# Layer 1's FFN by seven products, with the next layer's modulation on VectorE in two portions

## The chip, the cores and the metric

The kernel runs on one core of a Trainium2 chip. The metric is the device time of one execution in microseconds (us): three runs gave 3232.79, 3238.96 and 3241.5, so the median is 3238.96. Durations are read from one profiled execution. The engines are named as in the profile: PE multiplies matrices, DVE is VectorE, ACT ScalarE, POOL GpSimd, and SP only issues DMAs. DMAs also leave from POOL's and ACT's queues. Each engine's instructions run in a fixed order.

## The reference

Two layers of a diffusion backbone on 1024 latent tokens and 256 context tokens of width 1024. Each layer has modulation, three groups of attention heads, one output projection and a gated FFN of width 2816.

```
for i in range(DEPTH):                                    # DEPTH = 2
    mod, mod_c = silu(c) @ w_mod[i] + b_mod[i], silu(c_ctx) @ w_mod[i] + b_mod[i]
    sh1, sc1, g1, sh2, sc2, g2 = split(mod, 6)            # and sh1c ... g2c from mod_c
    h, hc = rms_norm(x)*(1+sc1)+sh1, rms_norm(xc)*(1+sc1c)+sh1c
    y, yc = token_mixers(h, hc, ...)      # gla, neighbourhood (na) and sliding-window (swa) attention, w_out
    x = x + g1*y
    x = x + g2 * ((silu(h2 @ w_gate[i]) * (h2 @ w_up[i])) @ w_down[i])    # h2: norm and sh2, sc2
    if i == 0:                                            # the context too, with g1c, g2c
        xc = xc + g1c*yc;  xc = xc + g2c * swiglu(norm(xc), ...)
return rms_norm(x, final_norm)
```

## The kernel before

Activations lie with the feature on the partitions, so a matrix of width 1024 is KD = 8 tiles; tokens fall into three blocks, B0 and B1 of 512 latents and BC of 256 context tokens. Every fp32 product is three matmuls of a high and a low part (`split`, L230 to 235: ACT copies the high part at L232, DVE subtracts at L234; `proj_T`, L436, whose matmul is L441). "Layer 1" is l = 0 in the code, "layer 2" is l = 1.

A layer runs: gla's projections (gp, gvp), gla's chain, into which the projections of swa and na are merged step by step (`merge`; the last of these are nqk, na's q and k), `swa_mix`, `na_mix`, `out_proj`, and the FFN. `na_mix` loads q, k (L803, L804) and windows of v (vw, L1039) into tiles of pool t_h, which hold the normalised input until the last projection has read it; it loads two bias tiles gm per half (L1058) and adds a table to them on POOL (L1062). A scheduler with its own timeline orders the instructions on each engine when the program is built; each engine and queue then runs in that order.

Layer 1's FFN is `ffn` (L1132). For each of NF = 22 tiles f it loads and splits three weight tiles, and for each block does 24 matmuls for gate, 24 for up, and 24 for down, whose eight sums DVE adds into x at once (L1157). Beside it `modulation_aside` (L332) computes the next layer's modulation: 96 rows of w_mod come over SP, POOL multiplies and adds them up (L342, L345, L346), DVE transposes and reduces the sums (L351, L352), and four PE matmuls (modt) bring them into place. At the end `last_norm` and the next layer's first norms follow.

Layer 2's FFN is another: `gates_seven` (L1228) replaces the eight block products of a two by two split by seven (22 jobs, product at L1286), with sums of weights made on POOL and DVE and sums of tokens on DVE; results a go to DRAM (aD). `down_blocks` (L1354) loads the rows of a back on POOL's queue (L1359), halves them on ACT and DVE (L1170, L1171), and sums over all 22 tiles in PSUM, one output tile m after the other (L1379), before the residual is added (L1398). This holds one block's a in SBUF, so w_down is loaded and split again for each block.

Of the kernel before, what the change touches and what calls it, by code (L numbers as in the profile page):

```python
# [87 lines left out]
def hybrid_layers(ctx: ExitStack, tc: tile.TileContext, A, K, out):  # L88
# [105 lines left out]
    xmD = [dr.tile([128, T], F32, name=f"xmD{k}") for k in range(KD)]  # L194
    aD = [dr.tile([128, T], F32, name=f"aD{f}") for f in range(NF)]
# [132 lines left out]

    def halves(t):
        return [t[:, 0:512], t[:, 512:1024]]  # L330

    def modulation_aside(l, u0, u1, part, sums, select):  # L332
        nu = u1 - u0
        pv4 = part[:, 0:32 * nu].rearrange("p (v b) -> p v b", v=2)
        for u in range(u0, u1):
            acc = sums()
            for k in range(KD):
                r = t_p("wm")[:, 0:512]
                SY.dma_start(r, A["w_mod"][l, 128 * k:128 * k + 128, 512 * u:512 * u + 512])
                for v in range(2):  # L340
                    if k == 0:
                        G.tensor_scalar(acc[v], r, sT[:, k, v:v + 1], None, ALU.mult)  # L342
                        continue
                    t = t_ev("mp")
                    G.tensor_scalar(t, r, sT[:, k, v:v + 1], None, ALU.mult)  # L345
                    G.tensor_tensor(acc[v], acc[v], t, ALU.add)  # L346
                if k % 2:
                    yield
            for v in range(2):
                t = t_ev("mtr")  # L350
                V.transpose(t, acc[v])  # L351
                V.tensor_reduce(pv4[:, v, 16 * (u - u0):16 * (u - u0) + 16], t.rearrange("p (b c) -> p b c", c=32),  # L352
                                axis=AX.X, op=ALU.add)
            yield
        sel = select()
        G.memset(sel, 0.0)
        for g in range(4):
            r = slice(32 * g, 32 * g + 32)
            V.tensor_copy(rev(sel[r], 0, [[160, 4], [1, 32]]), ident[r, r].unsqueeze(1).to_broadcast([32, 4, 32]))
        tp = p_c("modt")  # L360
        for q in range(4):
            PE.matmul(tp[:, 0:8 * nu], sel[:, 128 * q:128 * q + 128],
                      part[:, 0:32 * nu].rearrange("p (m q) -> p q m", q=4)[:, q], start=(q == 0), stop=(q == 3))
        V.tensor_tensor(modT[l][:, :, 4 * u0:4 * u1], tp[:, 0:8 * nu].rearrange("p (v j) -> p v j", v=2),
                        bmT[:, 48 * l + 4 * u0:48 * l + 4 * u1].unsqueeze(1).to_broadcast([128, 2, 4 * nu]), ALU.add)
        for w in range(2):
            if u0 <= 6 * w + 3 < u1:
                mod_vectors(l, w)
        yield


# [116 lines left out]
    def gla(l, hh, hl, ctx_out, before, given):  # L488
# [8 lines left out]
        def gproj(items, put, with_ctx, given=()):  # L497
            given = list(given)
            w = given + [None] * (len(items) - len(given))
            for blk in blks:  # L500
# [570 lines left out]
    def out_proj(l, blks):  # L1071
# [9 lines left out]
        def part(grp):  # L1081
# [6 lines left out]
            for m in range(KD):  # L1088
                w = wcols(A["w_out"][l], 128 * m)
                for o, n in grp:  # L1090
# [6 lines left out]
                    if len(blks) == 2:  # L1097
                        G.dma_start(xmD[m][:, o:o + n], x[m][:, o:o + n])
# [3 lines left out]
        def norms():  # L1102
            for blk in blks[:-1]:
# [3 lines left out]
                for k in range(KD):  # L1107
                    xv, pool = x[k][:, blk[0]:blk[0] + blk[1]], k % 2 == 1
                    if len(blks) == 2:
                        scaled(l, xv, r, k, yh, yl, blk)  # L1110
                    else:
                        modulate(l, 1, xv, r[:, :blk[1]], k, yh, yl, blk, pool)
                    yield
        run(merge(part(blks[-1:]), norms(), 1, 2))
        rs = block_rstd(ss, blks[-1])
        if len(blks) == 2:
            return x, yh, yl, rs
        rs = rs()
        return x, yh, yl, lambda: run(norm_block(l, 1, x, rs, yh, yl, blks[-1]))
# [12 lines left out]
    def ffn(l, x, hh, hl, blks, last):  # L1132
        ss, add = square_sums(x, blks)
        for f in range(NF):
            wg = wcols(A["w_gate"][l], 128 * f)
            wu = wcols(A["w_up"][l], 128 * f)
            r = t_raw("wd", [128, D])
            SY.dma_start(r, A["w_down"][l, 128 * f:128 * f + 128, :])
            wd = split(r, "wd", [128, D])
            for o, n in blks if f < NF - 1 else last:  # L1140
                pg = p_a("pg")
                proj_T(wg, hh, hl, (o, n), pg)
                pu = p_a("pu")
                proj_T(wu, hh, hl, (o, n), pu)
                a = t_w2("a")
                S.activation(a[:, :n], pg[:, :n], AF.Silu)  # L1146
                V.tensor_tensor(a[:, :n], a[:, :n], pu[:, :n], ALU.mult)
                ah, al = t_w2("ah", dt=F32R), t_w2("al", dt=F32R)
                S.activation(ah[:, :n], a[:, :n], AF.Copy)  # L1149
                V.tensor_tensor(al[:, :n], a[:, :n], ah[:, :n].bitcast(F32), ALU.subtract)  # L1150
                yield (f, (o, n), None)
                v = 1 if o == 1024 else 0
                for m in range(KD):
                    pd = either(p_b, p_c, "pd")
                    for i, (w, b) in enumerate(((wd[0], ah), (wd[0], al), (wd[1], ah))):
                        PE.matmul(pd[:, :n], w[:, m * 128:(m + 1) * 128], b[:, :n], start=(i == 0), stop=(i == 2))  # L1156
                    V.scalar_tensor_tensor(x[m][:, o:o + n], pd[:, :n], modT[l][:, v, 40 + m:41 + m],  # L1157
                                           x[m][:, o:o + n], ALU.mult, ALU.add)
                    if f == NF - 1 and last is blks:
                        add(m, (o, n))  # L1160
                yield (f, (o, n), ss)

# [11 lines left out]
    def token_sums(l, x, yh, yl, rs, ops):  # L1174
# [34 lines left out]
        for k in range(4):  # L1209
            t1, v22 = half(x[k], 0), half(x[k + 4], 1)  # L1210
            V.tensor_tensor(t1, v22, t1, ALU.subtract)
            j = 2 * k
# [9 lines left out]
        for k in range(4):  # L1222
            t2, v21 = half(x[k], 0), half(x[k + 4], 0)
            V.tensor_tensor(v21, v21, t2, ALU.subtract)
# [3 lines left out]
    def gates_seven(l, x, yh, yl, rs):  # L1228
        order = ("b11", "b21", "t1", "t3", "t2", "b22", "t4")
        jobs = [(f, w) for f in range(0, NF, 2) for w in ("w_gate", "w_up")]  # L1230
        early = 4
# [19 lines left out]
        def weights():  # L1251
# [4 lines left out]
            for j, (f, name) in enumerate(jobs):  # L1256
# [13 lines left out]
                yield made(s3)  # L1270
                yield made(a22)
# [3 lines left out]
        def product(i, bank, start):  # L1275
            w, b = ready.pop(0), ops[order[i]]
            new = next(feed, None)
            if new is not None:
                ready.append(new)
            for k in range(4):  # L1280
                wv = [t.rearrange("p (k f) -> p k f", f=128)[:, k] for t in w]
                for q, (p, m) in enumerate(((0, 0), (0, 1), (1, 0))):
                    pieces = b[k][m] if isinstance(b[k][m], list) else [b[k][m]]
                    n = 512 // len(pieces)
                    for c, v in enumerate(pieces):
                        PE.matmul(bank[:, n * c:n * c + n], wv[p], v, start=(start and k == 0 and q == 0),  # L1286
# [313 lines left out]
```

## Time and profile before

| what | value |
|---|---|
| median of three runs | 3238.96 us |
| the profiled execution | 3235.02 us, its span 3233.2 |
| PE busy | 3067.4 us, 95% |
| DVE, POOL, ACT busy | 53%, 34%, 32% |
| layer 1's FFN, 885 to 1835 us | PE busy for 938.75 of 950 |
| layer 2's FFN, 2515 to 3233 us | PE busy for 430.64 of 446, then 256.96 of 272 |

The span is the time from the first to the last instruction that the profile records; what the execution has beyond it lies around it. A window of the profile lists for a stretch of the span how long each engine was busy; PEclk is the granted share of TensorE's full clock. The chain is the succession of work that ended last, each piece with its start and length. A group of instructions by line has its busy time, the mean length of one in ns, the idle time in front of them and what ended that.

### The profile page before, as it was taken

Reading aid. Unit: us, or ns where it says so; the run is one execution under the profiler, and the core shown is the slowest. Engines: PE = TensorE matmul, PEld = TensorE weight load, DVE = VectorE, ACT = ScalarE, POOL = GpSimd, SP = SyncE. Lnnn points to the kernel's source line nnn. Section 1 sums busy time; section 2 is a strip of 40 time slices with the busy share of each in tenths; the row PEclk is TensorE's granted clock in tenths of the full one; section 3 lists DMA queues with packets and bytes.
Section 4 is the critical chain, followed back from the end, with each engine's and each line's share of the span. In section 5 each row is a group of like instructions: output and inputs, shape, how many; then the busy total and the mean of one; then the engine's idle time right before and its main releaser. Section 6 shows DMA issues by size and latency. Waiting matters only on the chain.

```text
span 3233.2 us, 50611 instructions
## 1 busy us (share of the span) xinstructions
PE 3067.4 (95%) x19726; PEld 2613.5 (81%) x19726; DVE 1726.4 (53%) x3431; ACT 1044.3 (32%) x1976; POOL 1087.8 (34%) x938
## 2 busy tenths in 40 slices
PE   7998999889999999999999899999989899999998
PEld 5887877677878888888888789887868688887877
DVE  3255444566675666666555724545766644444342
ACT  4332223455321111111111432224664444333231
POOL 1011020230189888887000101110411376655010
PEclk8999999999999999999999898999999999999999
DMA  7233455764312222222111223356555232225452
GB/s 251 84 125 104 126 160 156 209 186 155 92 62 72 82 79 82 79 82 66 40 40 38 76 66 98 95 155 184 148 172 171 69 101 79 79 85 170 143 187 80
DMA packets 371543, 365.80 MB, mean 113 GB/s; under 512 B 65100, under 2 KB 297512, under 8 KB 371304
## 3 DMA queue, kind: packets, MB, share of 16 engines
q1 hardware_dynamic: 358296, 318.79, 32.6%
q0 software_dynamic: 11856, 39.59, 3.8%
q10 hardware_dynamic: 1152, 4.19, 0.3%
q8 instruction: 155, 2.54, 0.3%
q14 instruction: 84, 0.69, 0.1%
HBM read 285.86 MB, written 76.64 MB: 112 GB/s over the span
## 4 chain that ended last, share of the span: by engine, by line
PE 72%; DMA 5%; DVE 4%; issue 3%; POOL 2%; ACT 1%; SPq 0%; DVEq 0%; ACTq 0%; POOLq 0%
PE q L1286 10%; PE pg L441 9%; PE pd L1156 9%; PE pu L441 9%; PE pd L1379 7%; PE op L441 6%; PE nqk L441 4%; PE ptp L849 3%; PE swp L448 2%; PE gp L441 1%; PE nao L863 1%; PE swo L863 1%; DMA wm<-in_w_mod_dram 1%; PE nvp L448 1%; PE gvp L448 1%
## 5 line engine op out<-in xcount | busy, mean ns | idle before, releaser
L1157 DVE SCALAR_TENSOR_TENSOR x<-pd,modT,x 128x512 f32<-128x512 f32 (+1 forms) x528 | 317.9, 655 | 195.0 <-PE pd L1156 192.9
L345 POOL TENSOR_SCALAR mp<-wm,sT 128x512 f32<-128x512 f32 x168 | 283.8, 1701 | 42.0 <-DVE mpart L352 35.9
L1286 PE MATMUL q<-yh,ws 128*128 128x512 f32 (+1 forms) x1056 | 282.9, 356 | 4.4 <-DVE us L1346 2.6
L1379 PE MATMUL pd<-ha,wdh 128*128 128x512 f32 (+1 forms) x748 | 225.2, 384 | 5.3 <-ACT ha L1170 2.2
L346 POOL TENSOR_TENSOR macc<-macc,mp 128x512 f32<-128x512 f32 x168 | 224.1, 1360 | 0.0
L830 ACT ACTIVATE P<-P,m 128x640 f32<-128x640 f32 (+2 forms) x216 | 167.2, 775 | 137.4 <-DVE m L826 131.4
L1286 PEld LDWEIGHTS q<-yh,ws 128*128 128x128 f32 x1056 | 183.3, 190 | 34.8 <-ACT ws L1170 5.6
L234 DVE TENSOR_TENSOR wcl<-wr,wch 128x1024 fp32r<-128x1024 f32 x98 | 140.7, 1435 | 124.1 <-ACT wch L232 122.5
L441 PE MATMUL pg<-yh,wch 128*128 128x512 f32 (+1 forms) x528 | 187.9, 356 | 1.0 <-ACT a L1146 1.0
L441 PE MATMUL pg<-yl,wch 128*128 128x512 f32 (+1 forms) x528 | 187.9, 356 | 0.0
L441 PE MATMUL pg<-yh,wcl 128*128 128x512 f32 (+1 forms) x528 | 187.4, 355 | 0.0
L441 PE MATMUL pu<-yl,wch 128*128 128x512 f32 (+1 forms) x528 | 187.1, 354 | 0.0
L441 PE MATMUL pu<-yh,wcl 128*128 128x512 f32 (+1 forms) x528 | 187.0, 354 | 0.0
L441 PE MATMUL pu<-yh,wch 128*128 128x512 f32 (+1 forms) x528 | 186.9, 354 | 0.0
L232 ACT ACTIVATE wch<-wr 128x1024 fp32r<-128x1024 f32 x100 | 106.0, 1060 | 245.3 <-PE pg L441 89.9
L1156 PE MATMUL pd<-al,wdh 128*128 128x512 f32 (+1 forms) x528 | 184.9, 357 | 0.0
L1156 PE MATMUL pd<-ah,wdl 128*128 128x512 f32 (+1 forms) x528 | 184.7, 357 | 0.0
L1286 PE MATMUL q<-yl,ws 128*128 128x512 f32 (+1 forms) x528 | 173.8, 356 | 0.4 <-DVE yl L1189 0.4
L1379 PEld LDWEIGHTS pd<-ha,wdh 128*128 128x128 f32 x748 | 139.9, 192 | 35.2 <-ACT ha L1170 3.8
L849 PE MATMUL ptp<-ident,P 128*128 128x128 f32 x984 | 144.5, 286 | 10.0 <-DVE pT L855 7.8
L1156 PE MATMUL pd<-ah,wdh 128*128 128x512 f32 (+1 forms) x528 | 148.6, 356 | 0.3 <-ACT ah L1149 0.3
L1379 PE MATMUL pd<-ha,wdl 128*128 128x512 f32 (+1 forms) x374 | 143.5, 384 | 0.8 <-DVE wdl L234 0.7
(351 smaller groups left out, 7809.9 us busy)
## 6 DMA issues: line engine op xcount, KB each, us to landing
wm<-in_w_mod_dram SPq DMA_DIRECT2D x96, 256.0 KB
wr<-in_w_gate_dram SPq DMA_DIRECT2D x46, 512.0 KB
wr<-in_w_up_dram SPq DMA_DIRECT2D x46, 512.0 KB
wm<-in_w_mod_dram POOLq DMA_DIRECT2D x32, 512.0 KB, 4.7
wr<-in_w_out_dram SPq DMA_DIRECT2D x32, 512.0 KB
wr<-in_w_down_dram SPq DMA_DIRECT2D x32, 512.0 KB
k<-naD SPq DMA_DIRECT2D x48, 320.0 KB
gm<-in_const_nam_dram SPq DMA_DIRECT2D x24, 576.0 KB
```

Source lines behind the costliest of these rows:

```text
L232: S.activation(h, raw, AF.Copy)
L234: engine.tensor_tensor(l, raw, h.bitcast(F32), ALU.subtract)
L345: G.tensor_scalar(t, r, sT[:, k, v:v + 1], None, ALU.mult)
L346: G.tensor_tensor(acc[v], acc[v], t, ALU.add)
L441: PE.matmul(pt[:, :n], a[:, k, :], b[k][:, o:o + n], start=(k == 0 and i == 0), stop=(k == KD - 1 and i == 2))
L448: PE.matmul(pt[:, :n], a[k][:, t * 128:(t + 1) * 128], b[:, k % 2, c0:c0 + n], start=(k == 0 and i == 0), stop=(k == KD - 1 and i == 2))
L830: exps[:] = [S.activation(P, P, AF.Exp, bias=m[:, i:i + 1], scale=-1.0, accum_out=sums[:, i:i + 1])]
L849: line[:] = [PE.transpose(tp[:, (cc * 2 + i) * 128:(cc * 2 + i + 1) * 128], pr[i][:, (c + cc) * 128:(c + cc + 1) * 128], ident)]
L1156: PE.matmul(pd[:, :n], w[:, m * 128:(m + 1) * 128], b[:, :n], start=(i == 0), stop=(i == 2))
L1157: V.scalar_tensor_tensor(x[m][:, o:o + n], pd[:, :n], modT[l][:, v, 40 + m:41 + m], x[m][:, o:o + n], ALU.mult, ALU.add)
L1286: PE.matmul(bank[:, n * c:n * c + n], wv[p], v, start=(start and k == 0 and q == 0), stop=(k == 3 and q == 2), skip_group_check=not start)
L1379: PE.matmul(pt[:, 0:n], w[i][:, f - f0, :], hs[f][b][:, c0:c0 + n], start=(f == 0 and q == 0), stop=(f == NF - 1 and q == 2))
```

## The change

Layer 1 now uses the seven products too. `gates_seven` takes the context along: its 256 columns are multiplied plainly by the four weight pieces a11, a12, a21 and a22, into a bank of their own, 48 matmuls a job, and the results are stored over SP. Since a bank more is in use, three jobs start early instead of four.

`down_next` is the new second half: blocks B0, B1 and BC one after the other, each with all weights of w_down loaded and split again; rows of the next x leave from ACT's queue, sums of squares go along. In the context block `norms()` fetches those rows for B0 and B1 on POOL's queue and normalises them beside the products, so that layer 2 starts its gp on B0. The context's own norm is layer 2's first job. `out_proj` stores its x to DRAM in both layers.

`modulation_aside` on POOL goes. `modulation_behind` does the products on DVE, one operation for a multiplication with its addition, and takes rows of w_mod over POOL's queue. Portion 1 (512-column pieces 0 to 3 of w_mod, for latents and context) runs beside the blocks B0 and B1 of down. Portion 2 (pieces 4 to 11, for latents only) runs in layer 2 as every third step of the projections.

```diff
+    def modulation_behind(l, u0, u1, row, sums, wide, ahead, every):
...
+                G.dma_start(r, A["w_mod"][l, 128 * k:128 * k + 128, 512 * u:512 * u + 512])
...
+            for v in range(nv):
+                if k == 0:
+                    V.tensor_scalar(acc[v], r, sT[:, k, v:v + 1], None, ALU.mult)
+                else:
+                    V.scalar_tensor_tensor(acc[v], r, sT[:, k, v:v + 1], acc[v], ALU.mult, ALU.add)
+            if k == KD - 1:
+                for v in range(nv):
+                    t = wide("mtr")[:, 0:512]
+                    V.transpose(t, acc[v])
+                    V.tensor_reduce(pv4[:, v, 16 * (u - u0):16 * (u - u0) + 16],
+                                    t.rearrange("p (b c) -> p b c", c=32), axis=AX.X, op=ALU.add)
+            if k % every == every - 1:
+                yield
...
+    def down_next(l):
+        def sums(m, hs, n, pt):
+            for f0 in range(0, NF, KD):
+                nf = min(KD, NF - f0)
+                r = t_raw("wr", [128, KD, 128])
+                SY.dma_start(r[:, 0:nf], A["w_down"][l][128 * f0:128 * (f0 + nf), 128 * m:128 * m + 128]
+                             .rearrange("(k p) f -> p k f", p=128))
+                w = split(r[:, 0:nf], "wd", [128, nf, 128])
+                for f in range(f0, f0 + nf):
+                    for q, (i, b) in enumerate(((0, 0), (0, 1), (1, 0))):
+                        PE.matmul(pt[:, 0:n], w[i][:, f - f0, :], hs[f][b], start=(f == 0 and q == 0),
+                                  stop=(f == NF - 1 and q == 2))
+        def take(f, o, n, dst):
+            r = t_w2("ar")[:, 0:n]
+            G.dma_start(r, aD[f][:, o:o + n])
+            halve(dst, r)
...
+            for m in range(KD):
+                pt = either(p_a, p_b, "pd")
+                sums(m, hs, n, pt)
+                V.scalar_tensor_tensor(xs[m], pt[:, 0:n], modT[l][:, v, 40 + m:41 + m], xs[m], ALU.mult, ALU.add)
+                if blk != BC:
+                    S.dma_start(xD[l + 1][:, m, o:o + n], xs[m])
...
+                if m in steps:
+                    for _ in range(steps[m]):
+                        next(aside, None)
...
+        aside = modulation_behind(l + 1, 0, 4, t_w2, sums_of, t_ev, 3, 2)
+        for o in (0, 512):
...
+            rqs.append(block((o, 512), hs, xs, aside, {m: 2 for m in range(1, 6)}))
...
+        def norms():
+            for rq, (o, n) in zip(rqs, (B0, B1)):
+                rs = across(rq, n)
+                for k in range(KD):
+                    xv = t_w2("xn")
+                    G.dma_start(xv, xD[l + 1][:, k, o:o + n])
+                    modulate(l + 1, 0, xv, rs, k, hh, hl, (o, n), False)
...
+        def context(w, half, bank):               # in gates_seven
+            for k in range(4):
+                for q, (p, y) in enumerate(((0, yh), (0, yl), (1, yh))):
+                    PE.matmul(bank[:, 0:C], w[k][p], y[4 * half + k][:, T:N], start=(half == 0 and k == 0 and q == 0),
+                              stop=(half == 1 and k == 3 and q == 2))
...
+            rest = modulation_behind(l, 4, 12, t_w2, lambda: [t_ev("macc")], t_ev, 1, 2)
         proj = merge(proj, rest, 2, 1)
         run(merge(chain(), proj, 1, 1, False))
         run(merge(seq(finish(), swa_mix(l, ctx_out)), proj, 1, 1))
         run(na_mix(l, ctx_out))
-        x, hh, hl, last_norm = out_proj(l, blks)
-        if not ctx_out:
-            gates_seven(l, x, hh, hl, last_norm)
+        x, hh, hl, rs = out_proj(l, blks)
+        gates_seven(l, x, hh, hl, rs, ctx_out)
+        if ctx_out:
+            hh, hl, last_norm = down_next(l)
```

The first place is POOL's order in layer 2 between the end of `swa_mix` and the start of `na_mix`: gm is a bias tile of na, yD a stored row of attention output. Before:

```order
L965 DMA yD_0_158<-ys_21537 64x512 x2
L1062 TENSOR_TENSOR gm_22211<-gm_22211,gt_22193 128x384 x3
L965 DMA yD_512_159<-ys_21751 64x512 x2
L965 DMA yD_0_158<-ys_21955 64x512 x2
L1062 TENSOR_TENSOR gm_22216<-gm_22216,gt_22202 128x384 x3
L1062 TENSOR_TENSOR gm_22358<-gm_22358,gt_22193 128x384 x3
L1062 TENSOR_TENSOR gm_22363<-gm_22363,gt_22202 128x384 x3
```

POOL's order at the same place now, with wm the rows of w_mod of portion 2:

```order
L1326 DMA wm_21807<-in_w_mod_dram 128x512
L1018 TENSOR_TENSOR gm_21927<-gm_21927,gt_21913 128x384 x3
L1326 DMA wm_21810<-in_w_mod_dram 128x512
L1018 TENSOR_TENSOR gm_22069<-gm_22069,gt_21904 128x384 x3
L1018 TENSOR_TENSOR gm_22074<-gm_22074,gt_21913 128x384 x3
L1326 DMA wm_21813<-in_w_mod_dram 128x512
L1326 DMA wm_21816<-in_w_mod_dram 128x512
L1326 DMA wm_21819<-in_w_mod_dram 128x512
L1326 DMA wm_21825<-in_w_mod_dram 128x512
```

The issues of rows now stand among the adds, and the last eleven (these four and seven more) behind nine adds that wait for loads of na.

The second place is PE's order at the end of `swa_mix` and the first tile of `na_mix`: swo are values of swa, sc and sl scores of na. Before:

```order
L863 MATMUL swo_22027<-pT_22120,vsw_20538 64x128 x4
L863 MATMUL swo_22027<-pT_22127,vsw_20538 64x128
L883 MATMUL rrt_22137<-ident,bc_22129 128x128 x4
L863 MATMUL swo_22027<-pT_22127,vsw_20538 64x128 x3
L849 MATMUL ptp_22275<-ident,P_22224 128x128
L849 MATMUL ptp_22275<-ident,P_22225 128x128
L808 MATMUL sc_22280<-k_4036_22163,q_22157 128x256
```

PE's order there now, with modt the four matmuls that end portion 2:

```order
L819 MATMUL swo_21549<-pT_21710,vsw_19709 64x128 x4
L819 MATMUL swo_21549<-pT_21717,vsw_19709 64x128
L839 MATMUL rrt_21727<-ident,bc_21719 128x128 x4
L819 MATMUL swo_21549<-pT_21717,vsw_19709 64x128 x3
L1359 MATMUL modt_21859<-mpart_17765,sel_21853 128x32 x4
L764 MATMUL sc_21934<-k_3830_21874,q_21868 128x256
L765 MATMUL sc_21934<-k_3831_21875,q_21868 128x256
```

Before, na's first tile (ptp, of its probabilities) was already under way between the last rows of swa; now no matmul of na stands in front of modt. The last nqk stands 38 rows further up in this order, with the scores and values of two swa tiles between.

The third place is DVE's order at the end of layer 1's FFN. Before, the last sums and the next layer's norm rows (nt, yl) take turns:

```order
L1157 SCALAR_TENSOR_TENSOR x_8274<-pd_17071,modT_113,x_8274 128x512
L419 TENSOR_SCALAR nt_17024<-nt_17024,av_116,modT_114 128x512
L424 SCALAR_TENSOR_TENSOR yl_8266<-nt_17029,modT_114,yh_8258 128x512
L1157 SCALAR_TENSOR_TENSOR x_8276<-pd_17087,modT_113,x_8276 128x512
L420 TENSOR_TENSOR yl_8265<-nt_17024,yh_8257 128x512
L422 SCALAR_TENSOR_TENSOR nt_17038<-x_8276,av_116,rs_17018 128x512
```

DVE's order in the context block of down now, about one output tile m:

```order
L234 TENSOR_TENSOR wdl_16370<-wr_16366,wdh_16368 128x768
L234 TENSOR_TENSOR wdl_16411<-wr_16407,wdh_16409 128x1024
L1398 SCALAR_TENSOR_TENSOR xm_15773<-pd_16305,modT_113,xm_15773 128x256
L378 SCALAR_TENSOR_TENSOR nt_16396<-xn_16394,av_116,rs_16291 128x512
L378 SCALAR_TENSOR_TENSOR nt_16402<-xn_16400,av_116,rs_16291 128x512
L234 TENSOR_TENSOR wdl_16441<-wr_16437,wdh_16439 128x1024
L1406 TENSOR_TENSOR ss_15775<-ss_15775,sq_16391 128x256
L380 SCALAR_TENSOR_TENSOR hl_15765<-nt_16396,modT_114,hh_15757 128x512
L380 SCALAR_TENSOR_TENSOR hl_15766<-nt_16402,modT_114,hh_15758 128x512
L234 TENSOR_TENSOR wdl_16471<-wr_16467,wdh_16469 128x768
```

Three splits of weights (wdl) now stand in every m, and the four norm operations of two rows between them.

## Rows read from the trace of the kernel before

**Rows 1.** The page: its first part (busy us, share, instructions), and the chain by line.

```profile
PE 3067.4 (95%) x19726; PEld 2613.5 (81%) x19726; DVE 1726.4 (53%) x3431; ACT 1044.3 (32%) x1976; POOL 1087.8 (34%) x938
...
PE q L1286 10%; PE pg L441 9%; PE pd L1156 9%; PE pu L441 9%; PE pd L1379 7%; PE op L441 6%; PE nqk L441 4%; PE ptp L849 3%; PE swp L448 2%; PE gp L441 1%; PE nao L863 1%; PE swo L863 1%; DMA wm<-in_w_mod_dram 1%; PE nvp L448 1%; PE gvp L448 1%
```

**Rows 2.** Windows by stage: us, PE, PEld, DVE, ACT, POOL, PEclk, DMA, GB/s.

```profile
885.00:1835.00 950.00, 938.75 (x4884) 807.50 (x4883) 588.01 (x865) 167.91 (x249) 560.78 (x379) 0.99 0.21 68
...
2515.00:2961.00 446.00, 430.64 (x2124) 364.58 (x2122) 218.27 (x266) 179.37 (x309) 261.16 (x177) 0.98 0.27 85
2961.00:3233.00 272.00, 256.96 (x1186) 211.48 (x1186) 108.55 (x141) 80.09 (x123) 34.31 (x53) 0.97 0.47 150
```

**Rows 3.** Windows inside the stages, columns as above.

```profile
2221.00:2316.00 95.00, 85.72 (x841) 72.03 (x839) 66.26 (x229) 58.34 (x142) 14.94 (x20) 1.00 0.61 163
2316.00:2420.00 104.00, 93.64 (x913) 79.86 (x912) 68.51 (x221) 65.65 (x147) 29.39 (x34) 0.96 0.58 167
...
1802.00:1855.00 53.00, 42.95 (x200) 35.01 (x199) 42.23 (x65) 23.42 (x39) 11.46 (x13) 0.88 0.28 102
...
2585.00:2909.00 324.00, 323.49 (x1611) 275.82 (x1612) 150.41 (x172) 128.98 (x222) 207.31 (x140) 0.99 0.27 86
...
2962.00:3105.00 143.00, 140.25 (x596) 112.84 (x597) 64.98 (x79) 48.78 (x68) 28.65 (x45) 0.98 0.56 177
```

**Rows 4.** The chain in order of time: start, length, what.

```profile
915.62 5.44 PE pg L441 x24
...
931.94 2.87 PE pg L441 x24
...
957.01 5.44 PE pg L441 x24
...
1854.38 46.02 PE gp L441 x192
...
2585.51 323.20 PE q L1286 x1608
```

**Rows 5.** Timeline of PE where the first FFN begins: start, length, what.

```profile
886.69 0.28 PE L441 MATMUL pg<-yh,wch 128*128 128x256 f32 x1
```

**Rows 6.** The instructions on tile gp in layer 2, one kind of three.

```profile
L441 PE MATMUL gp<-yh,wch x112: 277/389/797, 1802.4 to 1899.6; 128*128 128x512 f32 x96, 128*128 128x256 f32 x16
```

**Rows 7.** Waits of PE at layer 2's FFN start: total, times, longest.

```profile
PE q L1286 <- ACT ws L1170: 6.4, 1, 6.4
```

**Rows 8.** DMAs of the page's part 6, and the landing of L1359's.

```profile
wm<-in_w_mod_dram POOLq DMA_DIRECT2D x32, 512.0 KB, 4.7
...
DMA to landing us min/median/max: 3.2/5.1/8.9
```

**Rows 9.** Groups by line, 2962 to 3215 us: busy, mean ns, idle before.

```profile
L234 DVE TENSOR_TENSOR wdl<-wr,wdh 128x1024 fp32r<-128x1024 f32 x30 | 36.7, 1224 | 47.0 <-ACT wdh L232 46.1
...
L232 ACT ACTIVATE wdh<-wr 128x1024 fp32r<-128x1024 f32 x30 | 31.7, 1059 | 77.6 <-PE pd L1379 64.9 <-DMA wr<-in_w_down_dram 6.9 <-DMA out_dram<-fo 4.1
...
L1359 POOL DMA_DIRECT2D ar<-aD x40 | 21.6, 540 | 103.3 <-DVE ha L1171 100.4 <-DMA ar<-aD 1.9
...
L1398 DVE SCALAR_TENSOR_TENSOR xm<-pd,modT,xm 128x512 f32<-128x512 f32 x15 | 11.2, 750 | 28.2 <-PE pd L1379 27.9 <-DMA xm<-xmD 0.3
```

**Rows 10.** Groups of POOL and of DVE, 885 to 1835 us.

```profile
L345 POOL TENSOR_SCALAR mp<-wm,sT 128x512 f32<-128x512 f32 x168 | 283.8, 1701 | 42.0 <-DVE mpart L352 35.9 <-DMA wm<-in_w_mod_dram 4.3 <-DVE yl L420 1.1
...
L351 DVE STREAM_TRANSPOSE mtr<-macc 128x512 f32<-128x512 f32 x24 | 16.8, 701 | 0.0
```

**Rows 11.** The instructions on tiles nqk and swo: count, ns, first and last start.

```profile
L441 PE MATMUL nqk<-yh,wch x120: 278/389/501, 2118.2 to 2219.7; 128*128 128x512 f32 x96, 128*128 128x256 f32 x24
...
L863 PE MATMUL swo<-pT,vsw x422: 272/273/324, 2220.8 to 2315.8; 128*64 128x128 f32 x141
```

**Rows 12.** Timelines of SP's queue and of POOL: start, length, what.

```profile
2227.18 15.43 SPq L1039 DMA_DIRECT2D vw<-vD  x15
...
2309.31 8.89 POOL L1062 TENSOR_TENSOR gm<-gm,gt 128x384 f32<-128x384 f32 x9 [7.51 <-PE sl L809]
```

More of the change, by code (lines that the diff above doesn't have):

```diff
@@ L325, in modulation @@
             yield
[L329 to L369, printed above, removed]
     def square_sums(x, blks):
@@ L1130, in parts @@
         V.scalar_tensor_tensor(dst[1], v, b, dst[0].bitcast(F32), ALU.add, ALU.subtract)
[L1132 to L1161, printed above, removed]
     def t_x(s, dt=F32R):
@@ L1273, in gates_seven, with take @@
         ready = [next(feed) for _ in range(3)]
-        def product(i, bank, start):
-            w, b = ready.pop(0), ops[order[i]]
+        def take():
+            w = ready.pop(0)
             new = next(feed, None)
@@ L1279, in product @@
                 ready.append(new)
+            return [[t.rearrange("p (k f) -> p k f", f=128)[:, k] for t in w] for k in range(4)]
+        def product(i, bank, start):
+            w, b = take(), ops[order[i]]
             for k in range(4):
-                wv = [t.rearrange("p (k f) -> p k f", f=128)[:, k] for t in w]
                 for q, (p, m) in enumerate(((0, 0), (0, 1), (1, 0))):
@@ L1347, in gates_seven, with rows @@
             done(j, 1)
-            product(6, pd, False)
+            if ctx_too:
+                bank = p_b("qc")
+                context(take(), 0, bank)
+            w = product(6, pd, False)
+            if ctx_too:
+                context(w, 1, bank)
+                context_done(j, 1, bank)
             V.tensor_tensor(result(j, 2), u2, pd, ALU.add)
             done(j, 2)
+    def modulation_behind(l, u0, u1, row, sums, wide, ahead, every):
+        nu, nv = u1 - u0, 2 if u0 == 0 else 1
+        part = wk.tile([128, 128], F32, tag="mac", name=nm("mpart"), bufs=1)
+        pv4 = part[:, 0:16 * nu * nv].rearrange("p (v b) -> p v b", v=nv)
+        todo = [(u, k) for u in range(u0, u1) for k in range(KD)]
+        def rows():
+            for u, k in todo:
+                r = row("wm")[:, 0:512]
+                G.dma_start(r, A["w_mod"][l, 128 * k:128 * k + 128, 512 * u:512 * u + 512])
+                yield r
+        feed, ready, acc = rows(), [], None
+        for u, k in todo:
+            while len(ready) < ahead:
+                r = next(feed, None)
+                if r is None:
+                    break
+                ready.append(r)
+            r = ready.pop(0)
+            if k == 0:
+                acc = sums()
+            for v in range(nv):
+                if k == 0:
+                    V.tensor_scalar(acc[v], r, sT[:, k, v:v + 1], None, ALU.mult)
+                else:
+                    V.scalar_tensor_tensor(acc[v], r, sT[:, k, v:v + 1], acc[v], ALU.mult, ALU.add)
[7 more added lines that the diff above has]
+                yield
+        sel = wide("sel")[:, 0:512]
+        V.memset(sel, 0.0)
+        for g in range(4):
+            r = slice(32 * g, 32 * g + 32)
+            V.tensor_copy(rev(sel[r], 0, [[160, 4], [1, 32]]), ident[r, r].unsqueeze(1).to_broadcast([32, 4, 32]))
+        tp = p_c("modt")
+        n = 4 * nu * nv
+        for q in range(4):
+            PE.matmul(tp[:, 0:n], sel[:, 128 * q:128 * q + 128],
+                      part[:, 0:4 * n].rearrange("p (m q) -> p q m", q=4)[:, q], start=(q == 0), stop=(q == 3))
+        V.tensor_tensor(modT[l][:, 0:nv, 4 * u0:4 * u1], tp[:, 0:n].rearrange("p (v j) -> p v j", v=nv),
+                        bmT[:, 48 * l + 4 * u0:48 * l + 4 * u1].unsqueeze(1).to_broadcast([128, nv, 4 * nu]), ALU.add)
+        w = 0 if u0 == 0 else 1
+        for v in range(nv):
+            V.scalar_tensor_tensor(av[l][:, w, v], modT[l][:, v, 24 * w + 8:24 * w + 16], 1.0,
+                                   pv[:, 16 + 16 * w + 8 * l:24 + 16 * w + 8 * l], ALU.add, ALU.mult)
+        yield
```

153 lines of the change are left out of this document (96 added, 57 removed).

## The prediction

> **What bounds the kernel now.** I read the page's first part, then the chain by line, then the chain in order of time, and last the windows of the stages that the change touches. The page has PE busy for 3067.4 of 3233.2 us, DVE for 53%, POOL for 34%, and the chain's dearest lines are the FFN products of both layers [rows 1]. In layer 1's FFN PE is busy for 938.75 of 950 us [rows 2]: that stage lasts as long as its matmuls, so fewer of them are worth their time there. Layer 2's middle is another case: from the last projections to the end of swa_mix PE works 85.72 of 95 us, then in na_mix 93.64 of 104 [rows 3]. There a load or a row of VectorE that comes late is felt at the end.
>
> In the chain 24 pg matmuls of 512 columns take 5.44 us and 24 of 256 take 2.87 [rows 4]: 0.2267 and 0.1196 each. One matmul on all three blocks costs 2 x 0.2267 + 0.1196 = 0.573.
>
> **Layer 1's FFN, before.** From its first matmul at 886.69 [rows 5] to the end of layer 2's gp at 1854.38 + 46.02 = 1900.40 [rows 4] there are 1013.7 us. One f is 72 matmuls on each block, 72 x 0.573 = 41.26; the chain has 957.01 - 915.62 = 41.39 from one f to the next [rows 4], 910.5 for 22. gp has three kinds of 96 matmuls of 512 and 16 of 256 [rows 6], 71.0. What is left, 32, is loss, nearly all where the last block's sums, its norm and gp follow on each other: PE is busy for 42.95 of 53 us there, at a granted clock of 0.88 [rows 3].
>
> **Gate and up, after.** Each of 22 jobs has 7 products of 12 matmuls of 512, and 48 of 256 for the context: 84 x 0.2267 + 48 x 0.1196 = 24.78, 545.2 in all, where 22 x 48 x 0.573 = 605 stood: -60. That jobs of this kind hold such a rate is seen in layer 2: 96 matmuls a job (72 of 512, 24 of 256) are 19.19 by the prices above, and 1608 of them, 16.75 jobs, take 323.20 [rows 4], 19.30 a job. Its stage lasts 446 [rows 2] against 22 x 19.19 = 422: 24 lost, most of it at the start, where the longest single wait is 6.4 for ScalarE's first pieces [rows 7]. Here three early jobs hold 3 x (24 x 0.2267 + 48 x 0.1196) = 33.5 us of products for that time, layer 2's four 21.8. I take 22 (14 to 28).
>
> **Down, after.** 8 x 22 x 3 x 0.573 = 302.5, as before. Its losses are new to this layer, and layer 2's rows bound them: 596 matmuls, 135 us, in the first 143 [rows 3], so 8 lost about the first block; 7 from B0 to B1, the rest of what its stage of 272 [rows 2] has over 239.4 of products and the last norm's share; 6 from B1 to the context, 3 for transfers. In the context block weights may bind: it loads all of w_down again, 24 groups for 8 x 66 x 0.1196 = 63.1 of PE, and has two raw buffers, each held from issue until DVE's split. A transfer of 512 KB takes 4.7 [rows 8], ScalarE's part 1.06, DVE's 1.22 [rows 9]: 6.98 for two in flight, 3.49 a group. The third group, of six, comes to three quarters, 2.62: 16 x 3.49 + 8 x 2.62 = 77, 14 over PE. With two STTs of 0.75 [rows 9] ahead of each split it is 4.24 and 3.37, 95, 32 over; with prefetch that holds, 0. DVE's order there has two or four STTs of norm rows between splits (order of DVE in the section on the change): I take 18. Down's losses: 42.
>
> gp stays 71.0, with 4 in front of it. Sum 545.2 + 22 + 302.5 + 42 + 71.0 + 4 = 986.7: -27. With nothing lost in the context block and 14 in gates it is -53; with 32 there, 28 in gates and 6 more at the ends of blocks, -1.
>
> **Modulation, portion 1, and what goes.** POOL's 168 products of 1.70 us [rows 10] and the adds that belong to them go; they lay under PE, so nothing is gained. Portion 1 is 64 STTs of some 0.75 and 8 transposes of 0.70 [rows 10] with reduces that I take at as much, 59 us of DVE, beside B0's and B1's 239 of products. DVE has 48 splits (54), 44 halves at half a split (27) and 16 sums (12) there: 152 in all, so nothing. Without that cover it would cost as far as a split waits behind two steps, 1.5 us at a time, 15 for ten. xD's store at layer 2's head goes, and its rows leave from ScalarE's queue under PE: nothing either way.
>
> **Portion 2, at the seam from swa_mix to na_mix.** Here the change adds a wait. 64 rows of w_mod on POOL's queue and 64 STTs are dealt out among layer 2's projections; the projections last longer in the order, and the last nqk stands only two swa tiles before the end of swa (orders of PE and POOL in the section on the change). Before, nqk's last matmul began at 2219.7 and swo's at 2315.8 [rows 11]. 422 of the swo fall into 95 us [rows 11], 20 a tile, 4.5 us each: now PE is through some 8.5 us after the last nqk, which I call +0. na's q, k and v take the tiles that it frees. On SP the last 15 of 16 vw began 7.5 us after it and took 15.43 [rows 12], so gm's loads leave at +23.5 and land, at the 5.1 of a row of aD [rows 8], at +29. POOL's adds of gm stand in front of the last 11 rows of w_mod: three triples, nine adds of 0.99 [rows 12] and one row's issue between, done at +38.5. Six buffers are free: issues of 0.54 [rows 9] and landing bring the sixth row at +47, slots come free from +44.9, and the last row lands at +53.4; its STT, transpose, reduce and sel end at +56. PE's order has modt, which needs them, in front of na's first scores. So PE stands from +8.5 to +56: 47. At least it is 37 (gm in by +20), at most 60 (rows at 8.9).
>
> Against that: the swa tiles that now have projections beside them lose less of the 9.3 us of [rows 3], 6 back; na starts with its loads all there, 4 back of 10.4. The chain of gla, ahead, has less to fill it with: one step in three of what is merged into it is now without matmuls, +7. The middle comes to +44; at the most 60 with 5 more of chain, +65; with the wait hidden, 0 to +5.
>
> **A rule against the queue.** The rows of aD, issued from POOL while DVE halves and splits, landed in 3.2 to 8.9 us, 5.1 in the middle [rows 8]. The Trainium skill, "SBUF — State Buffer", section "SBUF: two separate sides", says that GpSimd itself writes the descriptors of a DMA issued from its queue, through a port that VectorE's operations can lock it out of, so that such a DMA seems slow. The trace has the spread and not its reason. If it bites, both batches at the seam land at 8.9 and not at 5.1, 2 x 3.8 = +7.6.
>
> **Sum.** -27 + 44 = +17: 3235.02 + 17 = 3252 for the profiled run (span 3233.2, 1.8 around it). The three runs have a median 3.9 above it: 3256.
>
> **Rivals.**
> *Seam hidden* (0.30; the one that is faster): rows and na's loads are in before swa ends, and the middle costs +3. It decides when the last row of w_mod lands by +10. For it: the DMA engines are busy for 0.61 of that time [rows 3], and swa's last tiles may themselves run slower. Against: three queues in a row (SP's vw, POOL's adds, the rows). 3239 - 27 + 3 = 3215.
> *Context block starved* (0.16): weights and norm rows hold each other up; the xn rows come on POOL's queue, and a late one stops the split behind it. FFN gives -5 and not -27, and gla's chain loses 7 more: 3256 + 22 + 7 = 3285. It decides at over 4.2 us a group. For it: 3.4 of splits and 3.0 of STTs of 7.9 us of PE per m. Against: layer 2's first block of down has DVE at 65 of 143 [rows 3], and PE keeps on.
> *The rate doesn't hold* (0.07): the fifth weight piece a21 and the context's results make a job wait 0.7 us: 22 x 0.7 = 15, 3271. Layer 2's jobs have POOL busy 207 and DVE 150 of 324 us [rows 3], so there is room.
> *Slow rows*, as above (0.05): 3256 + 7.6 = 3264.
>
> **How the numbers follow.** The forecast has 0.42, its own range 3239 to 3275. Under 0.3%, 10 us, a measurement of this kernel can't be told from no change: faster is below 3229, slower above 3249. Of the forecast 0.04 falls to faster, 0.16 to same, 0.22 to slower; of the hidden seam 0.27 and 0.03 (same); the others have 0.03 same and 0.25 slower. Sums: 0.31, 0.22, 0.47. The range 3205 to 3284 leaves out a third of the hidden seam and half of the starved block.
>
> **What would show it.** A job of layer 1's gates at 24.8 to 25.3 us; the context block of down at 63 (prefetch holds), 77 to 82 (mine) or over 95; a hole of PE of over 35 us in front of modt, ended by DVE, with POOL's adds of gm ahead of the last rows. No hole means the seam is hidden; a hole that a wait of another kind ends, that I have named the wrong queue. Wrong altogether would be a job over 27, or FFN above 1014.

## The result, and the profile after

The changed kernel takes 3328.53 us in the median of four runs (3318.81 to 3335.92), the kernel before 3240.23: a ratio of 1.028, 95% interval 1.0264 to 1.0297. It is slower, the sign forecast, by 88 us and not by 17. The profiled execution took 3335.92, its span 3334.1. It was the slowest of the four, so the stretches below add up to a span 101 us longer and not to 88. PE is busy for less than before; this is the first line of the page, against [rows 1]:

```profile
PE 3036.3 (91%) x19470; PEld 2583.6 (77%) x19470; DVE 1672.4 (50%) x3278; ACT 1201.7 (36%) x2258; POOL 876.6 (26%) x931
```

So waiting grew. Windows of the changed kernel, columns as in [rows 2]: the gates of layer 1, blocks B0 and B1 of down, its context block; then gla's chain with swa's and na's projections, the time between swa and na, and na.

```profile
890.00:1452.00 562.00, 553.73 (x2920) 476.09 (x2918) 270.38 (x317) 202.72 (x353) 254.42 (x180) 0.99 0.23 71
1452.00:1705.00 253.00, 246.20 (x1074) 200.96 (x1073) 157.94 (x224) 82.94 (x117) 54.83 (x95) 0.99 0.67 210
1705.00:1789.00 84.00, 70.60 (x546) 67.48 (x544) 53.28 (x76) 39.02 (x55) 11.82 (x22) 0.98 0.68 202
...
1910.00:2165.00 255.00, 217.06 (x1964) 195.71 (x1964) 142.53 (x339) 56.28 (x123) 48.50 (x70) 0.85 0.42 124
2325.00:2394.00 69.00, 2.52 (x14) 2.28 (x12) 22.02 (x36) 0.35 (x1) 19.82 (x30) 0.53 0.79 215
2394.00:2520.00 126.00, 98.72 (x937) 85.14 (x936) 73.82 (x241) 70.33 (x157) 26.71 (x30) 0.88 0.55 162
```

The FFN's three windows are as full as forecast. Below them PE stands for 38 of 255 us, for all of 69 at a granted clock of 0.53 (near the lower of its two levels, 1.2 of 2.4 GHz), and for 27 of 126. The tiles gp, nqk and swo give the borders, against [rows 6, 11]:

```profile
L397 PE MATMUL gp<-hh,wch x112: 283/389/629, 1789.3 to 1866.5; 128*128 128x512 f32 x96, 128*128 128x256 f32 x16
...
L397 PE MATMUL nqk<-hh,wch x120: 277/389/504, 2153.5 to 2314.6; 128*128 128x512 f32 x96, 128*128 128x256 f32 x24
...
L819 PE MATMUL swo<-pT,vsw x456: 272/273/324, 2163.8 to 2325.0; 128*64 128x128 f32 x152
```

| stretch | before | after | difference |
|---|---|---|---|
| start to the end of gp | 1900.4 | 1867 | -33 |
| end of gp to the last swo | 415.4 | 458 | +43 |
| last swo to the first matmul of na, on its own | hidden | 69 | +69 |
| from there (before: from the last swo) to out_proj | 107.8 | 125.8 | +18 |
| out_proj to the end | 809.6 | 814.6 | +5 |

In the first of the two middle stretches the last nqk now begins at 2314.6, 10 us before the end of swo, as the order had shown. What waits in gla's chain is in the waits of PE and then of POOL and DVE, 1910 to 2165 us (total, times, longest):

```profile
PE ket L593 <- DVE ke L589: 9.6, 5, 3.1
PE bp L572 <- DMA lac<-laD: 5.9, 3, 4.7
PE op L635 <- DVE sx L618: 4.9, 5, 1.9
PE at L628 <- DVE am L649: 4.7, 3, 3.1
```

```profile
...
POOL wm L1326 <- PE op L635: 37.0, 3, 18.8
...
POOL am L646 <- DVE macc L1342: 11.0, 4, 7.4
```

```profile
DVE macc L1342 <- DMA wm<-in_w_mod_dram: 14.0, 8, 4.0
```

POOL stands with a row's issue until PE's op has read one of the chain's tiles and so freed a buffer of t_w2; DVE then stands for the row. am and ke belong to the chain and stand behind them. At the seam, the timelines of SP, of POOL and of PE and the chain answer to [rows 12] (in brackets the idle time before, and what ended it):

```profile
2324.95 24.38 SPq L995 DMA_DIRECT2D vw<-vD  x16
2349.74 1.34 SPq L1014 DMA_DIRECT2D gm<-in_const_nam_dram  x3
```

```profile
2355.51 2.88 POOL L1018 TENSOR_TENSOR gm<-gm,gt 128x384 f32<-128x384 f32 x3 [16.91 <-issue]
2358.34 0.57 POOL L1326 DMA_DIRECT2D wm<-in_w_mod_dram  x1
2358.93 5.72 POOL L1018 TENSOR_TENSOR gm<-gm,gt 128x384 f32<-128x384 f32 x6
2364.61 2.67 POOL L1326 DMA_DIRECT2D wm<-in_w_mod_dram  x5
```

```profile
2391.77 1.92 PE L1359 MATMUL modt<-mpart,sel 128*128 128x32 f32 x8 [66.48 <-DVE sel L1355]
```

```profile
2366.74 14.89 DMA wm<-in_w_mod_dram
2381.72 0.76 DVE macc L1342
...
2382.77 5.46 DMA wm<-in_w_mod_dram
...
2391.77 1.92 PE modt L1359 x8
```

That is the chain forecast, link by link: vw, gm, nine adds, the last rows, modt. Two links are longer. The 16 vw go out in 24.38 us, where 15 took 15.43 before, so gm's loads leave 35 us after the last nqk and not 23.5. The last rows take up to 14.89 us and not 5.1, while na's loads for its second pair of heads are under way. In na a second hole follows. POOL's adds wait for the second half of the biases; the store of ys stands behind them on POOL's queue; and ScalarE's copy pT waits for the buffer of t_w2 that this store holds, and PE for pT (windows, the chain, PE's and ScalarE's waits from 2420 to 2446):

```profile
2424.00:2434.00 10.00, 0.04 (x2) 0.00 (x0) 0.32 (x3) 0.00 (x0) 4.76 (x6) 0.72 0.89 255
2434.00:2444.00 10.00, 0.00 (x0) 0.00 (x0) 0.00 (x0) 0.09 (x1) 1.48 (x3) 0.50 1.02 248
```

```profile
2424.89 4.09 DMA gm<-in_const_nam_dram
...
2431.13 3.78 POOL gm L1018 x4
2434.91 8.91 DMA yD<-ys
```

```profile
ACT pT L809 <- DMA yD<-ys: 21.6, 1, 21.6
...
PE nao L819 <- ACT pT L809: 20.3, 1, 20.3
```

### The profile page after: what moved, and what is told of

It reads as the page before. It is cut to its first block, busy times and chain, and to the rows that moved or that the text cites. A ratio compares the mean times of both kernels' runs of the same rounds, so it can differ in the third digit from the quotient of the medians.

```text
span 3334.1 us, 50957 instructions
## 1 busy us (share of the span) xinstructions
PE 3036.3 (91%) x19470; PEld 2583.6 (77%) x19470; DVE 1672.4 (50%) x3278; ACT 1201.7 (36%) x2258; POOL 876.6 (26%) x931
## 4 chain that ended last, share of the span: by engine, by line
PE 76%; DMA 9%; DVE 5%; issue 4%; POOL 2%; ACT 2%; SPq 1%; ACTq 0%; DVEq 0%; POOLq 0%
PE q L1217 22%; PE pd L1380 7%; PE pd L1485 7%; PE op L397 6%; PE nqk L397 5%; PE gp L397 5%; PE swp L404 4%; PE qc L1225 4%; DMA wm<-in_w_mod_dram 3%; PE ptp L805 3%; PE nvp L404 3%; PE gvp L404 2%; PE swo L819 1%; PE nao L819 1%; DMA wr<-in_w_down_dram 1%
## 5 line engine op out<-in xcount | busy, mean ns | idle before, releaser
L1217 PE MATMUL q<-yh,ws 128*128 128x512 f32 (+1 forms) x1760 | 515.0, 370 | 5.9 <-DVE us L1303 2.7
L1217 PE MATMUL q<-t,ws 128*128 128x512 f32 x1320 | 321.1, 394 | 17.8 <-ACT t L1080 6.9
L1217 PEld LDWEIGHTS q<-t,ws 128*128 128x128 f32 x1320 | 248.4, 190 | 71.2 <-ACT t L1080 7.7
L1091 DVE TENSOR_TENSOR ws<-s,ws 128x512 fp32r<-128x512 f32 x176 | 184.1, 1047 | 176.3 <-ACT ws L1090 173.4
L1091 DVE TENSOR_TENSOR ws<-wr,ws 128x512 fp32r<-128x512 f32 x154 | 143.2, 933 | 195.6 <-ACT ws L1090 195.4
L234 DVE TENSOR_TENSOR wdl<-wr,wdh 128x1024 fp32r<-128x1024 f32 (+1 forms) x120 | 138.7, 1157 | 190.7 <-ACT wdh L232 162.3
L1380 PE MATMUL pd<-ha,wdh 128*128 128x512 f32 x704 | 220.1, 393 | 5.6 <-ACT wdh L232 2.9
L1217 PEld LDWEIGHTS q<-yl,ws 128*128 128x128 f32 x880 | 160.7, 190 | 25.0 <-DVE yl L1109 0.7
L1250 POOL TENSOR_TENSOR us<-us,gs 128x512 f32<-128x512 f32 x88 | 139.8, 1597 | 113.2 <-DVE us L1257 102.8
L1225 PE MATMUL qc<-yh,ws 128*128 128x256 f32 x704 | 140.4, 283 | 0.0
```

What stands on the lines that cost most here:

```text
L234: engine.tensor_tensor(l, raw, h.bitcast(F32), ALU.subtract)
L1091: V.tensor_tensor(dst[1], v, dst[0].bitcast(F32), ALU.subtract)
L1217: PE.matmul(bank[:, n * c:n * c + n], w[k][p], v, start=(start and k == 0 and q == 0), stop=(k == 3 and q == 2), skip_group_check=not start)
L1225: PE.matmul(bank[:, 0:C], w[k][p], y[4 * half + k][:, T:N], start=(half == 0 and k == 0 and q == 0), stop=(half == 1 and k == 3 and q == 2))
L1250: G.tensor_tensor(c, c, gates.pop((j - 1, i)), ALU.mult)
L1380: PE.matmul(pt[:, 0:n], w[i][:, f - f0, :], hs[f][b], start=(f == 0 and q == 0), stop=(f == NF - 1 and q == 2))
```

## The experiments

Theory 1: portion 2 in layer 2's middle is the whole loss, because its rows hold up queues and buffers that PE waits for. The rivals: the new FFN, the spreading of the projections, DVE's time, the DMA engines. Times are medians of four or more runs; the kernel before had 3236.9 to 3239.3 beside them.

**Without portion 2.** `rest = iter(())`, constants in modT and av.

> Leaves out portion 2 of the modulation: its columns of modT and av are filled with constants. Theory 1 (portion 2 in layer 2's middle is the whole loss, about 43 us in gla's chain and swa, 69 at the seam, 18 in na): the middle goes back to the kernel before, nqk ends near 2190, and the time is about 3200 (3190 to 3212), faster than before by the 33 us of the FFN. Rival (the new second half of layer 1's FFN, its stores and its other order of gp make the chain slow): 3290 or more, with PE at a granted clock under 0.9 from 1920 to 2120 us as now.

3198.59, ratio 0.9884 (0.9859 to 0.9908): the FFN is worth 38 us, and portion 2 cost 130. The 38 are net: in the profiled executions gp ends 46 us earlier than before, and from there to the end it is 10 us longer.

**Empty steps.** `rest = iter((None,) * 33)`.

> Leaves out the work of portion 2 (constants in its place) but keeps its 33 steps, empty, among the projections, so the projections are spread as in the changed kernel. If the rows and STTs hold up DVE and POOL (theory 1), the chain loses at most 10 us against the run without steps, and only the late nqk is left, a hole of 25 to 30 us in front of na: about 3235. If the spreading itself costs the chain its cover (rival), the chain from 1867 to the end of swa takes some 455 us as now: about 3270 to 3290.

3207.16, a miss: no hole is left in front of na. The spreading costs 9 us, little more than the runs spread (3191 to 3206 without steps, 3204 to 3211 with them). And it doesn't move nqk: its last matmul begins 96 us before the last swo, as before the change. The stretches from 53 us behind gp on, changed kernel and then empty steps:

```profile
1920.00:2120.00 200.00, 167.62 (x1610) 149.23 (x1612) 116.93 (x289) 37.62 (x87) 34.51 (x58) 0.83 0.40 118
```

```profile
1912.00:2112.00 200.00, 188.63 (x1751) 169.00 (x1750) 101.96 (x263) 45.39 (x98) 20.96 (x34) 0.96 0.40 113
```

The DMA share is the same, 0.40; PE's work is not.

**Products without rows, rows without products.** The first reads the resident unit matrix in place of r, the second lets DVE touch 32 columns of each row.

```diff
-                r = row("wm")[:, 0:512]
+                if nv == 1:
+                    yield ident.unsqueeze(1).to_broadcast([128, 4, 128])
+                    continue
```

> Leaves out the loads of portion 2: all its 64 products, transposes, reduces and modt are made as in the changed kernel, on the resident unit matrix in place of rows of w_mod. If rows and their buffers are the price (theory 1), nqk ends some 95 us before swa does, as without portion 2, and 64 STTs cost 5 to 15 us beside empty steps: 3210 to 3225. If DVE's time in its queue is the price (rival), the chain stays as long as now: 3270 and above.

> Leaves out the products of portion 2, but for 32 of the 512 columns of each row: all rows are loaded over POOL's queue into t_w2 as in the changed kernel, and DVE touches each briefly. Theory 1: nearly all of the loss stays, nqk ends within 15 us of swa, a hole of 50 to 70 us in front of na: 3300 to 3330. Rival (DVE's time): 3225 to 3250.

3223.49 and 3331.55. Against 3207.16 with empty steps DVE's 57 us of work cost 16, the rows alone 124. The last nqk of the first begins 107 us before the last swo; that of the second 14, and the hole in front of na is 92 us, more than the 50 to 70 expected. nqk of both:

```profile
L397 PE MATMUL nqk<-hh,wch x120: 277/389/497, 2089.3 to 2194.8; 128*128 128x512 f32 x96, 128*128 128x256 f32 x24
```

```profile
L397 PE MATMUL nqk<-hh,wch x120: 274/389/500, 2135.9 to 2296.1; 128*128 128x512 f32 x96, 128*128 128x256 f32 x24
```

**What of a row costs.** From the run with rows only: rows on SP's queue; 16 columns a row; 16 columns in three buffers of their own.

```diff
-                r = row("wm")[:, 0:512]
-                G.dma_start(r, A["w_mod"][l, 128 * k:128 * k + 128, 512 * u:512 * u + 512])
+                r = row("wm")[:, 0:512] if nv == 2 else wk.tile([128, 16], F32, tag="wmp", name=nm("wm"), bufs=3)
+                c = 512 if nv == 2 else 16
+                G.dma_start(r[:, 0:c], A["w_mod"][l, 128 * k:128 * k + 128, 512 * u:512 * u + c])
```

> Leaves out the products of portion 2 but for 32 columns a row, as the run with rows only (3331.55), and issues the rows from SP's queue. If POOL's queue is the price, the chain wins back 30 us or more: below 3300. If it is the buffers of t_w2 or the bytes, it stays within 15 of that run, or is worse, since SP's other loads then stand behind rows that wait for a buffer: 3315 to 3360. I expect the second.

> Leaves out the products of portion 2 but for 16 columns a row, and loads only these 16 columns, 8 KB a row in place of 256 KB; as many DMAs from POOL, and a buffer of t_w2 for each. If bytes are the price: 3220 to 3240. If the buffers of t_w2 are the price (they are held as long, and the last nqk stands as late in PE's order as in the changed kernel), most of the loss stays: 3280 to 3320. I expect the second, with a shorter hole at the seam, as the last rows land sooner.

> As the run before, with the small rows in three buffers of their own. The same loads from the same queue; only t_w2 is left to gla's chain. If the buffers are the price: 3205 to 3222, nqk ending some 95 us before swa. If POOL's queue or the count of DMAs is the price, it stays within 15 us of the run before.

3303.52, 3299.91 and 3233.51. SP's queue gives back 28 us, which I had not expected: POOL's queue has a part. A thirty-second of the bytes gives back 32. The same small rows out of t_w2 give back 66 more, and nqk is early again, 106 us before the last swo: for small rows the buffers are the largest part. The last run still missed its range, by 12 us: 26 over empty steps are left.

Where in the middle each run loses its time, from the starts of the last gp, the first nqk, the last swo, the first nao (na's first values) and the first op of out_proj, in us of the profiled executions:

| run | gp to nqk | nqk to last swo | to first nao | to out_proj |
|---|---|---|---|---|
| before | 218 | 198 | 2 | 106 |
| changed kernel | 287 | 172 | 75 | 119 |
| without portion 2 | 220 | 203 | 2 | 105 |
| empty steps | 220 | 207 | 2 | 106 |
| products without rows | 231 | 212 | 2 | 106 |
| rows without products | 280 | 174 | 99 | 104 |
| the same, on SP's queue | 277 | 173 | 67 | 113 |
| 16 columns, in t_w2 | 281 | 176 | 57 | 116 |
| 16 columns, buffers of their own | 229 | 216 | 2 | 105 |

With rows in t_w2 the chain is some 50 us longer up to the first nqk, 35 to 40 come back as projections then lie beside swa, and the hole opens: most of what the buffers cost is paid at the seam. There, too, lies what the bytes cost. Full products without rows and short steps on rows in their own buffers end at the same length, 443 and 445 us from gp to the last swo against 427 with empty steps, so the length of DVE's operations doesn't set that rest.

**Other buffers at full size.** Rows in t_p, two ahead.

> Rows of portion 2 in buffers of pool t_p and loaded two ahead, instead of in t_w2, which gla's chain uses for its tiles. If the chain is late because POOL stands at a row's DMA until the chain frees a buffer, and DVE at a row just issued, the chain wins 20 to 35 us: about 3300. If it is late by the STTs themselves or by the spreading, there is no change: 3325 to 3335. The seam keeps its hole under both.

3339.68, a miss. In the chain it did what was expected, from gp's end to the first nqk 235 us and not 287 (220 without portion 2). But t_p holds swa's probabilities: nqk then takes 214 us, gp's end to the last swo 467 and not 458, and the seam 90. So no run has full rows in buffers that nothing else draws from:

```profile
2325.00:2415.00 90.00, 2.12 (x10) 2.04 (x10) 23.71 (x34) 0.14 (x1) 30.16 (x40) 0.53 0.68 182
```

**The rest of the steps in na.** `run(merge(na_mix(l, ctx_out), rest, 1, 1))`, and the projections' merge ends with them.

> Portion 2 is not run to its end before na: once the projections are used up, its last steps are merged with na_mix, so modt no longer stands in front of na's first scores. If the hole of 69 us is set by the chain vw, adds of gm, last rows, modt (theory 1), the part behind the adds goes, 25 to 35 us, and a hole of 30 to 40 stays for na's own loads: 3290 to 3305. If the hole is na's loads alone (rival), it stays at 60 or more: 3320 and above.

3321.59, a miss. The hole in front of na shrinks from 69 to 27 us, as theory 1 has it, but na with the rows in it takes 155 us and not 126 at a granted clock of 0.83 (0.88 in the changed kernel).

**By matmuls.** `rest = modulation(l, 4, 12, ...)` in both layers.

> Portion 2 by matmuls, as layer 1 does the same columns in its own middle (512 KB pieces into the weights' two raw buffers, 256 small matmuls, adds on DVE). If the loss is DVE's queue held by rows (theory 1), this loses only PE time of some 15 to 20 us and waits for raw buffers: 3215 to 3235. If any 16 MB of rows in that stage cost as much, because the DMA engines are short there (rival), 3270 or more.

3293.77, a miss, and within what the rival forecast. Its 512 KB pieces use the two raw buffers that na's tables gt need as well, and all 32 loads of gt leave behind the last piece, from 2352 on. In the hole PE first stands for pieces (mod are its products with them, the last modt begins at 2348.71) and then, with portion 2 done, for na's biases (window, PE's waits from 2300 to 2380, then the chain):

```profile
2305.00:2375.00 70.00, 15.95 (x170) 10.40 (x171) 8.22 (x32) 4.64 (x11) 18.00 (x22) 0.54 0.76 201
```

```profile
PE mod L310 <- DMA wm<-in_w_mod_dram: 32.4, 8, 7.4
PE sl L764 <- DVE m L782: 15.6, 1, 15.6
```

```profile
2308.34 18.04 DMA gm<-in_const_nam_dram
2326.39 4.79 SPq L995
```

Whether late pieces come from the raw buffers or from DMA engines busy for 0.76 isn't shown here.

**Beside gp, beside down.** Three or four steps as jobs of `before` at gp's blocks B0 and B1, the rest among the projections; or all of portion 2 behind portion 1, `{m: 3 for m in range(KD)}`.

> Most of portion 2 (21 of 33 steps) at the head of layer 2, beside gp on B0 and B1, where PE has 65 us of products and DVE little to do; the last 12 steps stay among the projections. Theory 1 (a row costs where it holds up a queue that PE waits for): nqk ends near 2200, no hole in front of na, a few us lost in the chain's first part: 3208 to 3225. Rival (the DMA engines or DVE's time are the price): the stage of gp lasts 30 us longer and nothing is won over the kernel before: 3235 and above.

> As the run before, with four steps at each place (28 of 33) and rows loaded three ahead, so that portion 2 ends before the projections of swa are far. Theory 1: a little better than with three, 3203 to 3218, unless 14 MB of rows are more than gp's 65 us can load, some 225 GB/s by what the stage around na's loads moved: then gp lasts 10 us longer, 3215 to 3225.

> Portion 2 beside the blocks B0 and B1 of layer 1's down, behind portion 1, three steps per output tile; nothing of it in layer 2's middle. Theory 1: middle as before, B0 and B1 have DVE busy for about 211 of 240 us and lose 5 to 15: 3205 to 3218. Rival (splits of weights wait behind STTs whose rows are late, as in the chain): B0 and B1 lose 40 or more, 3240 and above.

3255.98, 3246.87 and 3234.46, three misses, by 31, 22 and 16 us. With four steps gp lasts 97 us and not 78; how the rest divides wasn't followed. Beside down, B0 and B1 take 277 us and not 253:

```profile
1448.00:1725.00 277.00, 259.29 (x1075) 205.70 (x1074) 206.00 (x293) 81.09 (x108) 84.19 (x152) 0.96 0.77 249
```

DMA moves 249 GB/s there, against 210 with portion 1 alone.

**In the gates.** Two steps a job from the fourth on.

```diff
             product(3, pd, True)
+            if j >= 3:
+                next(rest, None)
+                next(rest, None)
```

> Portion 2 in layer 1's gates and up instead of layer 2's middle, two steps (four rows) a job from the fourth job on, rows on POOL's queue in t_w2. There DMA is busy for 0.23 and DVE for 270 of 562 us, and PE has 24.8 us of products a job that hang on a few sums only. Theory 1, a row costs where PE waits for what stands behind it: the pieces of weights that POOL makes stand behind rows, so it may cost up to 1 us a job: 3200 to 3222. Rival (16 MB of rows cost 36 to 50 us wherever they are put, as beside down and gp): 3235 to 3250.

> As the run before, with the rows on SP's queue. SP there issues only four loads of weights and some stores a job. Theory 1: POOL's sums no longer stand behind a row that waits for a buffer, so the gates keep 562 us and the kernel is as fast as without portion 2 within 10 us: 3197 to 3210. Rival: if a row that waits for a buffer on SP holds up the loads of weights behind it, the gates lose 20 us or more: 3220 and above.

3204.78 with POOL's queue, ratio to the kernel before 0.9904 (0.9886 to 0.9923), and 3215.73 with SP's. This beats the kernel before by 33 us, 1%, and the changed kernel by 124. It is 6 over leaving portion 2 out, within the spread of the two runs. The gates take 563 us with all of portion 2 in them, 562 without:

```profile
884.00:1447.00 563.00, 555.02 (x2926) 476.54 (x2924) 317.99 (x404) 201.53 (x352) 300.03 (x244) 0.99 0.32 101
```

That SP's queue isn't the better one here was not expected. Its gates take 8 us longer in the profiled executions, but the runs overlap (3203 to 3215 and 3208 to 3221), and the cause wasn't followed.

## Why the prediction was wrong

The sign was right, with a chance of 0.47 on it, and so were the seam's place and chain; the size was not: 3256 was forecast, at most 3284, and 3328.53 was measured.

*FFN.* From its first product to the end of gp 986.7 was forecast and 977 measured against 1013.7: -37 and not -27. The table's -33 counts 3.6 us lost in front of it; ten more runs that leave everything up to gp alone have -31 to -47 in that row. Gates, from the first q at 890.3, took 562 against 567; B0 and B1 253 against 254; gp 78 against 75. The context block took 83.4 against 81, with 9 us forecast about it that aren't seen. The cycle of two raw buffers was the right row: in that block SP's loads of weights stand 21.2 us for DVE's splits, and ScalarE's splits 27.9 for the loads. Portion 1 cost 7 us at most: PE is busy for 246 of the 253.

*The middle.* +44 was forecast, +130 measured, and here is the step that failed: "the projections last longer in the order", from steps dealt out, with a price of +7 for gla's chain and 6 back in swa. Up to the first nqk the chain lost 68 us and not 7; of this 26 came back beside swa: together +43, where I had +1. All was judged by which instructions stand beside which, and what a waiting row holds was put at nothing. Empty steps don't move nqk. Rows that wait hold buffers of t_w2, which gla's chain and swa share, and places in POOL's and DVE's queues; small rows make the chain as late in t_w2 (281 us to the first nqk) and not in buffers of their own (229). That full rows would do as well in buffers of their own isn't shown. The scheduler built that late nqk into PE's order, so the order showed the effect, and I named the wrong cause for it. Of the 43, 8 stay when portion 2 is left out, and their cause stays open. The upper bound of +65 is 62 by its own terms (60 + 7 + 5 - 6 - 4).

*The seam.* Its links were right, their lengths not: 69 us against 47. gm's loads left 11.6 us later than forecast, and from POOL's last add to modt it took 27 us and not 17.5, since I took each load at the length that it has alone. Beside rows of 16 columns the 16 vw went out in 16.27 us, beside full ones in 24.38. na's gain of 4 was a loss of 18, most of it the second hole (PE stands 22.0 us in na for ScalarE's pT, 4.9 before): POOL's queue and a buffer of t_w2 once more.

*The rivals.* A hidden seam fell. The starved context block fell: it kept near the forecast's rate. The seven products hold theirs, 562 us for 22 jobs. Slow rows came, by more than that rival's 8.9: at the seam rows landed in 9.0 us in the median and 14.89 at most. Of the reason that the Trainium skill gives, "SBUF — State Buffer", section "SBUF: two separate sides", the seam shows little. DVE was busy for 4.77 of the 14.89 us, so its operations can have held that row back for a third of them at most; the DMA engines were busy for 0.99 of them, which is nearer, though no run sets the two apart.

*Open.* The 8 us above; what sets the 16 to 18 us that full products without rows and short steps alike cost between gp and the last swo; and the 5 us behind out_proj, which are within the spread of the runs.

## What to carry to other kernels

A load that is dealt out beside another stage is priced by the buffer it holds there and by what stands behind its issue more than by its bytes (here 32 us) or by the work done on it (16); look up who else draws from the pool. When an order shows a row in a late place, ask what the scheduler made it wait for: the cause may be moved, not the row. Put side work where the bound engine's products hang on few things and buffers turn over quickly: the same 64 rows cost 130 us in the middle of layer 2 and some 6 in the gates.

## What was not expected of the hardware

Many short holes lowered the granted clock over a whole stage: in gla's chain it was 0.83 with PE busy for 168 of 200 us, and 0.96 with 189. A row of 256 KB landed in 3.1 us in the median between 1910 and 2320 us, and in 9.0 at the seam, beside na's loads.
